# The second mixer of a two-block transformer kernel, rewritten: stick heads first, dilated scores in three float32r passes

## The chip, the cores and the metric

The kernel runs on one core of one Trainium2 chip. The metric is the device time of one execution in microseconds; the kernel before took 3473.2 us (median of three runs, 3472.29 to 3477.33). TensorE (PE) multiplies matrices, with its weight loads shown apart (PEld); VectorE (DVE), ScalarE (ACT) and GpSimd (POOL) do elementwise work; SyncE (SP) issues the weight transfers.

## The reference, cut to what matters

A sequence of 512 tokens of width 1024 passes two blocks of two layers. The change touches the mixer of the second block, `hybrid_mixer`, once in each of two layers:

```python
proj = h @ w_in                                 # 1024 -> 5120
# dilated: 12 heads of 64, four in each of three groups (window, dilation); q, k roped
for g, (window, dilation) in enumerate(((128, 1), (512, 4), (2048, 16))):
    o[g], lse[g] = dilated_window_attention(q_d[g], k_d[g], v_d[g], window, dilation)
o_dil = sum(softmax(lse, axis=0) * o)           # over the groups: 4 heads of 64
# stick breaking, 4 heads of 64:
z = q_s @ k_s.T / 8
after = reverse_cumsum(log_sigmoid(-z)) - log_sigmoid(-z)   # over earlier keys
o_sb = (exp(log_sigmoid(z) + after) where key < query) @ v_s
y = sigmoid(gate_dil) * (o_dil @ w_proj_dil) + sigmoid(gate_sb) * (o_sb @ w_proj_sb)
return y @ w_out
```

Everything is float32. A float32r product runs in one pass but keeps fewer bits, so the dense products are made of three: each operand is split into a high and a low part, and hi·hi, hi·lo and lo·hi are summed.

## The kernel before

Weights come as chunks of 128 x 1024. SP loads each into `wraw`, ACT copies it to `whi` (L63) and DVE subtracts to `wlo` (L64). One feature tile (128 features x 512 tokens) is `fm_block`: 8 k-tiles of three matmuls (`mm3a`, L177 to L179), summed in a PSUM bank `pa`. Token tiles (`tm`, `mm3b`, L183 to L185) fill four banks `pb` at once. PSUM has eight banks in two tags of four; dense work holds one tag, background work the other.

`mix2` walks its projections: the dilated q and k (names q0 to q5, k0 to k5; each `evac` runs `rope`: a DVE shuffle and a DVE multiplication that read the bank `pa`, then two POOL instructions), the values (`tm`), the stick q and k (sq, sk), and 16 gate tiles g0 to g15. `dilated(half)` and `stick` are generators in a background list: after every k-tile of dense work `tick` adds 640 ns of credit, and the generator runs on while it has credit, each `yield` naming its cost. So the order of every engine's queue is fixed when the program is built. `drain` runs what is left of the list at a stretch, before the last four gate tiles.

`dilated(half)` holds two heads, one on partitions 0 to 63 and one on 64 to 127, and works on them one after the other (s = 0, 1): scores (`far` twice, `near` twice) as float32 matmuls, which PE runs as two instructions each; transposes `pm` for the maxima, `pmt` to spread them, Exp on ACT, and `pod` with the values. `stick` takes four heads one after the other: scores `pz`, then per key block Abs, Exp and Ln on ACT and one DVE instruction (L1103 to L1106), sums with a triangular matrix into `pz` again, Exp, and `pos`. At the end, for each of eight tiles n, two products `pp` are multiplied by the gates g(n) and g(8+n) on DVE (L952), added on POOL (L954) and split into y's two parts, the input of `w_out`.

Of the kernel before, what the change touches and what calls it, by code (L numbers as in the profile page):

```python
# [11 lines left out]
F32 = mybir.dt.float32  # L12
# [8 lines left out]
T = 512  # L21
# [70 lines left out]
class Block:  # L92
# [769 lines left out]
    def mix2(self, l, next_gain, final):  # L862
        nc, a, ph = self.nc, self.a, self.phase
        self.n_scr = 8
# [46 lines left out]
        def to_v0_vsb(t, ps):  # L911
            nc.scalar.activation(v[:, t, 0:2, 0::2], heads(ps[:, :256]), AF.Copy)
            nc.scalar.activation(v_sb[:, t], ps[:, 256:], AF.Copy)

        def to_v12(t, ps):
            nc.scalar.activation(v[:, t, 2:6, 0::2], heads(ps), AF.Copy)

        o_dil = (ph.tile([128, 2, T], F32R, name="od_hi"), ph.tile([128, 2, T], F32R, name="od_lo"))
        o_sb = (ph.tile([128, 2, T], F32R, name="os_hi"), ph.tile([128, 2, T], F32R, name="os_lo"))
# [17 lines left out]
        def split_sum():  # L937
            y.append(self.fm_parts("fm", 17))
            self.split_to(*y[-1], sums.pop(0))

        for c in range(4):
            i, w = self.st.take()
            for j in range(2):
                n = 2 * c + j
                acc = []
                for s, src in enumerate((o_dil, o_sb)):
                    ps = self.bank(tag, "pp")
                    for k in range(2):
                        q = ((j * 2 + s) * 2 + k) * 128
                        self.mm3a(ps, [x[:, q:q + 128] for x in w], [x[:, k] for x in src], k == 0, k == 1)  # L950
# [19 lines left out]
    def dilated(self, half, fm, v, o_dil):  # L970
        nc = self.nc
        den, num = self.spare("den"), self.spare("num")
        mm = lambda out, lhsT, rhs: nc.tensor.matmul(out, lhsT, rhs, start=True, stop=True, skip_group_check=True)  # L973
        pair = self.window_kq[:, None, :].to_broadcast([128, 2, 256])
        for s in range(2):
            p = slice(64 * s, 64 * s + 64)
            q = [fm[f"q{2 * g + half}"][p] for g in range(3)]
            k = [fm[f"k{2 * g + half}"][p] for g in range(3)]
            mx = self.small.tile([128, 3, 4], F32, name="mx", bufs=2)
            lo, hi = slice(0, 64), slice(64, 128)  # L980

            def near(i):

                ps = self.bank(self.bg_tag, "pst")
                for b in (2 * i, 2 * i + 1):
                    n = min(256, T - b * 128)
                    mm(ps[:, (b % 2) * 256:(b % 2) * 256 + n], k[0][:, b * 128:(b + 1) * 128], q[0][:, b * 128:b * 128 + n])
                x = self.scratch("es")
                if i == 0:
                    f = lambda a: a.rearrange("p (a b) -> p a b", a=2)  # L990
                    nc.vector.tensor_add(f(x), f(ps), pair)
                else:
                    nc.vector.tensor_add(x[:, :384], ps[:, :384], self.window_kq3)
                return x

            def far(g, mask):
                ps = self.psum.tile([128, 4, 128], F32, name="pst", tag=self.bg_tag)
                for t in range(NT):
                    mm(ps[:, t], self.tokens(k[g], g, t), self.tokens(q[g], g, t))
                x = self.scratch("es").rearrange("p (t i) -> p t i", t=4)  # L1000
                nc.vector.tensor_add(x, ps, mask[:, None, :].to_broadcast([128, 4, 128]))
                return x

            def turned(blocks):
                ps = self.bank(self.bg_tag, "pm")
                for i, x in enumerate(blocks):
                    nc.tensor.transpose(ps[:, i * 128:(i + 1) * 128], x, self.ident)
                return ps

            def far_max(g, x):  # L1010
                ps = turned([x[:, t] for t in range(NT)])
                nc.vector.reduce_max(mx[:, g], ps.rearrange("p (t i) -> p t i", t=4), axis=AX)

            x1 = far(1, self.causal_kq)
            yield 900
            x2 = far(2, self.resid_kq)
            yield 900
            far_max(1, x1)
            yield 900
            x0 = near(0)  # L1020
            yield 900
            far_max(2, x2)
            nc.vector.tensor_max(mx[:, 1], mx[:, 1], mx[:, 2])
            yield 900
            x3 = near(1)
            yield 900
            of = lambda b, i: (x0 if b < 2 else x3)[:, (b % 2) * 256 + i * 128:(b % 2) * 256 + (i + 1) * 128]
            m = self.spare("m")
            ps = self.bank(self.bg_tag, "pmt")
            for t in range(NT):  # L1030
                nc.tensor.transpose(self.tokens(ps, 1, t), mx[:, 1, t:t + 1].to_broadcast([128, 128]), self.ident)
            nc.scalar.activation(m, ps, AF.Copy)
            yield 900
            ps = turned([of(0, 1), of(1, 0), of(1, 1), of(2, 0)])
            nc.vector.reduce_max(mx[:, 0, 1:3], ps.rearrange("p (t i) -> p t i", t=2), axis=AX)
            ps = turned([of(2, 1), of(3, 0), of(0, 0)])
            nc.vector.reduce_max(mx[:, 0, 3:4], ps[:, :256], axis=AX)
            nc.vector.reduce_max(mx[:, 0, 0:1], ps[:, 256:384], axis=AX)
            yield 1800
            ps = self.bank(self.bg_tag, "pmt")  # L1040
            for t in range(NT):
                nc.tensor.transpose(self.tokens(ps, 0, t), mx[:, 0, t:t + 1].to_broadcast([128, 128]), self.ident)
            nc.vector.tensor_max(m, m, ps)
            yield 900

            mt = m.rearrange("p (i t) -> p t i", t=4)
            tiles = []
            for g, x in ((1, x1), (2, x2)):
                nc.vector.tensor_sub(x, x, mt)
                nc.scalar.activation(x, x, AF.Exp, scale=0.125)  # L1050
                tiles.append([(x[:, t], t, g, None) for t in range(NT)])
            for x, bs in ((x0, (0, 1)), (x3, (2, 3))):
                n = 0
                tiles.append([])
                for b in bs:
                    w = min(256, T - b * 128)
                    nc.vector.tensor_sub(x[:, n:n + w], x[:, n:n + w], m[:, b * 128:b * 128 + w])
                    tiles[-1].append((x[:, n:n + w], b, 0, slice(b * 128, b * 128 + w)))
                    n += w
                nc.scalar.activation(x[:, :n], x[:, :n], AF.Exp, scale=0.125)  # L1060
            yield 2500
            po = self.bank(self.bg_tag, "pod")
            for i, tile_ in enumerate(tiles):
                for j, (x, t, g, cols) in enumerate(tile_):
                    lhsT = v[:, t, 2 * g + half, s:s + 2].rearrange("p a d -> p (a d)")
# [217 lines left out]
```

## Time and profile before

| | |
|---|---|
| median of the runs | 3473.2 us |
| profiled execution: its own time / its span | 3472.38 / 3470.6 us |
| PE busy | 98% of the span |
| chain that ended last | 90% PE, 4% DVE, 2% ACT |
| mean granted TensorE clock | 0.988 of full speed |
| background work of `mix2`, first dilated score to the end of the last stick head | 1665.72 to 1886.49 us and 2788.82 to 3009.48 us |

The profile is of one execution. A matmul's end is modelled, so two matmuls that follow each other overlap in it; what a group of them costs is read from its first start to the first start behind it.

### The profile page before, as it was taken

The page shows a single profiled execution, that of the slowest core. Times are in us where ns is not written, and L with a number is a line of the kernel's source. Part 1 is how long each engine was busy: PE and PEld are TensorE (multiplying, and loading weights), DVE is VectorE, ACT ScalarE, POOL GpSimd, SP SyncE. Part 2 cuts the span into 40 slices and gives each one's busy share as a digit, 9 for nine tenths or more (in the row PEclk, how much of TensorE's full clock was granted, in tenths as well). Part 3 has the DMA queues.
Part 4 walks back from the last instruction along what each step waited for, and adds up shares of the span by engine and source line. Part 5 has one row for each costly group of instructions (what it writes and reads, how often), then busy time and mean ns, then how long its engine had stood idle before and what let it go on. Part 6 is the DMA issues. An engine that isn't in the chain of part 4 may idle for free.

```text
span 3470.6 us, 39287 instructions
## 1 busy us (share of the span) xinstructions
PE 3389.0 (98%) x15984; PEld 2798.7 (81%) x15984; DVE 1512.5 (44%) x1989; ACT 1172.4 (34%) x1862; POOL 355.8 (10%) x412
## 2 busy tenths in 40 slices
PE   8899999989999999999999999999999999999999
PEld 6678888767888888888876888888888887688887
DVE  4655542565554343324543533333332454353332
ACT  4344432334443332222235332223222223533221
POOL 2421100242110000003200100000000320010000
PEclk9999999999999999999999999999999999999999
DMA  4122332312333233333111233323332311123332
GB/s 161 44 74 92 99 114 85 113 49 68 98 103 111 81 99 97 103 97 102 61 55 56 91 103 97 103 86 103 97 103 97 102 55 61 55 92 102 97 103 79
DMA packets 87188, 311.97 MB, mean 90 GB/s; under 512 B 10368, under 2 KB 11072, under 8 KB 87008
## 3 DMA queue, kind: packets, MB, share of 16 engines
q1 hardware_dynamic: 85536, 305.17, 27.1%
q0 software_dynamic: 1472, 4.30, 0.4%
q8 instruction: 126, 2.06, 0.2%
q14 instruction: 54, 0.44, 0.0%
HBM read 307.32 MB, written 2.10 MB: 89 GB/s over the span
## 4 chain that ended last, share of the span: by engine, by line
PE 90%; DVE 4%; ACT 2%; POOL 1%; issue 1%; DMA 1%; DVEq 0%; POOLq 0%; ACTq 0%; SPq 0%
PE pa L177 18%; PE pa L178 18%; PE pa L179 18%; PE pb L183 10%; PE pb L184 10%; PE pb L185 10%; PE pst L973 1%; PE pz L1079 1%; DVE wlo L64 1%; PE ph L220 1%; PE pod L1067 1%; ACT whi L63 1%; PE pos L1079 1%; DVE xn L210 1%; PE psc L662 0%
## 5 line engine op out<-in xcount | busy, mean ns | idle before, releaser
L64 DVE TENSOR_TENSOR wlo<-wraw,whi 128x1024 fp32r<-128x1024 f32 x556 | 706.9, 1273 | 1139.5 <-ACT whi L63 1138.1
L177 PE MATMUL pa<-h_hi,whi 128*128 128x512 f32 (+1 forms) x3072 | 1172.4, 382 | 2.0 <-ACT h_hi L162 2.0
L178 PE MATMUL pa<-h_lo,whi 128*128 128x512 f32 (+1 forms) x3072 | 1148.2, 374 | 2.7 <-DVE h_lo L163 2.7
L179 PE MATMUL pa<-h_hi,wlo 128*128 128x512 f32 (+1 forms) x3072 | 1147.3, 373 | 0.0
L63 ACT ACTIVATE whi<-wraw 128x1024 fp32r<-128x1024 f32 x556 | 585.2, 1053 | 723.1 <-PE pb L185 560.0
L177 PEld LDWEIGHTS pa<-h_hi,whi 128*128 128x128 f32 x3072 | 583.2, 190 | 112.4 <-issue 10.8
L179 PEld LDWEIGHTS pa<-h_hi,wlo 128*128 128x128 f32 x3072 | 582.5, 190 | 102.7
L178 PEld LDWEIGHTS pa<-h_lo,whi 128*128 128x128 f32 x3072 | 583.7, 190 | 97.2 <-DVE h_lo L163 4.3
L183 PE MATMUL pb<-whi,hid_hi 128*128 128x512 f32 x1056 | 411.8, 390 | 0.0
L184 PE MATMUL pb<-wlo,hid_hi 128*128 128x512 f32 x1056 | 410.9, 389 | 0.0
L185 PE MATMUL pb<-whi,hid_lo 128*128 128x512 f32 x1056 | 410.9, 389 | 0.0
L185 PEld LDWEIGHTS pb<-whi,hid_lo 128*128 128x128 f32 x1056 | 198.3, 188 | 41.3
L183 PEld LDWEIGHTS pb<-whi,hid_hi 128*128 128x128 f32 x1056 | 198.3, 188 | 40.9
L184 PEld LDWEIGHTS pb<-wlo,hid_hi 128*128 128x128 f32 x1056 | 198.3, 188 | 40.7
L438 ACT ACTIVATE hid_hi<-act 128x512 fp32r<-128x512 f32 x88 | 55.6, 632 | 383.9 <-DVE act L449 383.9
L201 POOL TENSOR_TENSOR rs<-ss 128x1 f32<-128x1 f32 x44 | 11.9, 271 | 1605.7 <-ACT sqs L191 1605.7
L449 DVE TENSOR_TENSOR act<-act,pa 128x512 f32<-128x512 f32 x88 | 60.4, 687 | 210.4 <-PE pa L179 210.4
L458 DVE SCALAR_TENSOR_TENSOR cv<-pa,cw,cv 128x511 f32<-128x511 f32 (+1 forms) x176 | 131.5, 747 | 16.0 <-ACT cv L456 12.9
L445 ACT ACTIVATE act<-pa 128x512 f32<-128x512 f32 x88 | 52.5, 597 | 246.6 <-PE pa L179 246.6
L183 PE MATMUL pb<-whi,h_hi 128*128 128x512 f32 x256 | 102.2, 399 | 5.4 <-ACT vg L618 3.1
L184 PE MATMUL pb<-wlo,h_hi 128*128 128x512 f32 x256 | 101.4, 396 | 1.2 <-DVE wlo L64 1.2
L185 PE MATMUL pb<-whi,h_lo 128*128 128x512 f32 x256 | 101.3, 396 | 0.0
(269 smaller groups left out, 2916.1 us busy)
## 6 DMA issues: line engine op xcount, KB each, us to landing
wraw<-w_ffn SPq DMA_DIRECT2D x264, 512.0 KB, 3.6
wraw<-w_mix SPq DMA_DIRECT2D x160, 512.0 KB, 3.6
wraw<-w_mlp SPq DMA_DIRECT2D x132, 512.0 KB, 3.6
X<-x SPq DMA_DIRECT2D x4, 512.0 KB, 7.7
gain<-norm_ffn SPq DMA_DIRECT2D x4, 512.0 KB, 4.5
out<-xn SPq DMA_DIRECT2D x8, 256.0 KB, 2.0
gain<-norm_mix_pre SPq DMA_DIRECT2D x2, 512.0 KB, 5.7
rope_da<-c_rope SPq DMA_DIRECT2D x2, 512.0 KB, 8.2
```

The source lines that it names most:

```text
L63: self.nc.scalar.activation(hi, t, AF.Copy)
L64: self.nc.vector.tensor_sub(lo, t, hi.bitcast(F32))
L177: mm(ps, w[0], h[0], start=first, stop=False)
L178: mm(ps, w[0], h[1], start=False, stop=False)
L179: mm(ps, w[1], h[0], start=False, stop=last)
L183: mm(ps, h[0], w[0], start=first, stop=False)
L184: mm(ps, h[0], w[1], start=False, stop=False)
L185: mm(ps, h[1], w[0], start=False, stop=last)
L438: nc.scalar.activation(hid[0][:, f], h, AF.Copy)
L449: nc.vector.tensor_mul(g, g, ps)
L458: nc.vector.scalar_tensor_tensor(c[:, s:], ps[:, :T - s], cw[:, j, i:i + 1], c[:, s:], op0=OP.mult, op1=OP.add)
L1079: mm = lambda out, lhsT, rhs, first: nc.tensor.matmul(out, lhsT, rhs, start=first, stop=True, skip_group_check=True)
```

## The change

The order of the projections (and of the weight chunks in `arrange`) is turned: stick q and k first, in the halves form, with `stick` queued at once; then the first values, six dilated tiles, `dilated(0)`, the other values, six dilated tiles, `dilated(1)`, gates. A dilated tile is roped into a `raw` tile and, at least 4500 ns of credit later, split into two float32r parts, for groups 1 and 2 with the tokens regrouped by residue, so that the scores read columns that lie side by side. Scores are three float32r passes, alternating between the two heads on partitions 0 to 63 and 64 to 127; every step of `dilated` serves both heads. All these tiles, the outputs and y share one tag of 24 buffers (before: 17, and the outputs apart). Stick's and dilated's last steps wait in the list until the values are there.

```diff
@@ mix2
-        self.n_scr = 8
+        self.n_scr = 9
-        new_fm = lambda name: ph.tile([128, T], F32, name="fm" + name, tag="fm", bufs=17)
+        new_fm = lambda name, dt=F32: ph.tile([128, T], dt, name="fm" + name, tag="fm", bufs=24)
+        self.two = lambda name: (new_fm(name + "h", F32R), new_fm(name + "l", F32R))
         def dil(name):
+            g = int(name[1]) // 2
+            turned = lambda x: x.rearrange("p (i r) -> p i r", r=4) if g else x
+            grouped = lambda x: x.rearrange("p (r i) -> p i r", r=4) if g else x
             def evac(ps):
-                fm[name] = new_fm(name)
-                self.rope(fm[name], ps, self.ROPE16, rope[:, 0], rope[:, 1])
+                raw = new_fm("raw")
+                self.rope(raw, ps, self.ROPE16, rope[:, 0], rope[:, 1])
+                def split():
+                    parts = self.two(name)
+                    self.split_to(*[grouped(x) for x in parts], turned(raw))
+                    fm[name] = parts
+                    fm["at"] = self.clock
+                self.after(4500, split)
...
-        self.fm([dil("q0"), dil("q2"), dil("q4"), dil("k0")], halves=True)
-        self.fm([dil("k2"), dil("k4")])
+        self.fm([plain("sq0", 0.125), plain("sk0", 1.0), plain("sq1", 0.125), plain("sk1", 1.0)], halves=True)
+        self.bg.work.append(self.stick(fm, v_sb, o_sb))
         self.tm(KD, 512, v_rows(0), to_v0_vsb, tag, tail=1)
+        self.fm([dil(n) for n in ("q0", "q2", "q4", "k0", "k2", "k4")])
+        self.bg.work.append(self.dilated(0, fm, v, o_dil))
         self.tm(KD, 512, v_rows(1), to_v12, tag, tail=1)
-        self.bg.work.append(self.dilated(0, fm, v, o_dil))
         self.fm([dil(n) for n in ("q1", "q3", "q5", "k1", "k3", "k5")])
         self.bg.work.append(self.dilated(1, fm, v, o_dil))
-        self.fm([plain("sq0", 0.125), plain("sq1", 0.125), plain("sk0", 1.0), plain("sk1", 1.0)])
-        self.bg.work.append(self.stick(fm, v_sb, o_sb))
         self.fm([plain(f"g{j}", 1.0) for j in range(12)])
         self.drain()
...
-            y.append(self.fm_parts("fm", 17))
+            y.append(self.two("y"))
@@ dilated
+        def scored(ps, g, key, query):
+            q, k = fm[f"q{2 * g + half}"], fm[f"k{2 * g + half}"]
+            for j, (a, b) in enumerate(((0, 0), (0, 1), (1, 0))):
+                for s, p in enumerate(rows):
+                    mm(ps[s], k[a][p, key], q[b][p, query], j == 0, j == 2)
...
-                    mm(ps[:, t], self.tokens(k[g], g, t), self.tokens(q[g], g, t))
+                scored([x[:, t] for x in ps], g, c, c)
```

The first place is PE's queue in layer 1, where the first dilated scores begin (`pst`; a row before is four float32 matmuls, `fmq`/`fmk` the q and k tiles, h and l their parts). Before:

```order
L179 MATMUL pa<-h_hi,wlo 128x512
L973 MATMUL pst<-fmq_11707,fmk_11810 128x128 x4
L177 MATMUL pa<-h_hi,whi 128x512
L178 MATMUL pa<-h_lo,whi 128x512
L179 MATMUL pa<-h_hi,wlo 128x512
L973 MATMUL pst<-fmq_11743,fmk_11847 128x128 x4
L177 MATMUL pa<-h_hi,whi 128x512
```

After:

```order
L185 MATMUL pb<-whi,h_lo 128x512
L986 MATMUL pst<-fmq2h,fmk2h 128x128 x2
L986 MATMUL pst<-fmq2l,fmk2h 128x128 x2
L986 MATMUL pst<-fmq2h,fmk2l 128x128 x2
L986 MATMUL pst<-fmq2h,fmk2h 128x128 x2
L986 MATMUL pst<-fmq2l,fmk2h 128x128 x2
L986 MATMUL pst<-fmq2h,fmk2l 128x128 x2
```

A far group is now twelve such rows, a pair of heads in each. Before, a layer has four series of 13 background groups of `dilated` in PE's queue, after two series of 18.

The second place is PE's queue in layer 2 where the list is drained, from the last scores of the fourth stick head to the first gate tile behind. Before:

```order
L1079 MATMUL pz<-fmsq_20074,fmsk_20191 128x128
L1079 MATMUL pz<-ab,tri 128x512 x2
L1079 MATMUL pz<-ab,tri 128x384 x2
L1079 MATMUL pz<-ab,tri 128x256 x2
L1079 MATMUL pz<-sp_20917,tri 128x128 x2
L1079 MATMUL pz<-ab,tri 128x384 x2
L1079 MATMUL pz<-ab,tri 128x256 x2
L1079 MATMUL pos<-sw,v_sb 64x512
L1079 MATMUL pos<-sw,v_sb 64x384
L1079 MATMUL pos<-sw,v_sb 64x256
L1079 MATMUL pos<-sw,v_sb 64x128
L177 MATMUL pa<-h_hi,whi 128x512
```

After, at the last background matmuls of the layer:

```order
L986 MATMUL pod<-es,v 128x256 x2
L177 MATMUL pa<-h_hi,whi 128x512
L178 MATMUL pa<-h_lo,whi 128x512
L179 MATMUL pa<-h_hi,wlo 128x512
L986 MATMUL pod<-es,v 128x256
L986 MATMUL pod<-es,v 128x128
L177 MATMUL pa<-h_hi,whi 128x512
```

Behind these stand 213 dense matmuls of gate tiles: nothing is left to drain. Before, the whole fourth head stood with no dense matmul between its steps.

The third place is DVE's queue in layer 2 at the last dilated tile before a `tm` (k4 in both). Brackets name the engines whose semaphores a row waits for. Before:

```order
L499 STREAM_SHUFFLE sh<-pa 128x512 [waits PE_49]
L500 TENSOR_TENSOR fmk_19256<-pa,rope 128x512
L64 TENSOR_TENSOR wlo<-wraw,whi 128x1024 [waits DMAHW2_49,Activation_49]
L499 STREAM_SHUFFLE sh<-pa 128x512 [waits PE_49]
L500 TENSOR_TENSOR fmk_19293<-pa,rope 128x512
```

After:

```order
L1148 SCALAR_TENSOR_TENSOR sp_19950<-pz,sp_19950 128x512 [waits PE_49,Activation_49]
L1148 SCALAR_TENSOR_TENSOR sp_19951<-pz,sp_19951 128x384 [waits PE_49,Activation_49]
L1148 SCALAR_TENSOR_TENSOR sp_19952<-pz,sp_19952 128x256 [waits DVE_49,PE_49,Activation_49]
L1148 SCALAR_TENSOR_TENSOR sp_19951<-pz,sp_19951 128x128 [waits Activation_49]
L163 TENSOR_TENSOR fmk2l<-fmraw,fmk2h 128x128x4 [waits Activation_49]
L499 STREAM_SHUFFLE sh<-pa 128x512 [waits PE_49]
L500 TENSOR_TENSOR fmraw<-pa,rope 128x512
```

The rope of k4 now stands behind the fourth stick head's four DVE steps and the split of k2. On PE, six dense matmuls follow that head's scores, then the `tm`, three matmuls for each of its four banks; the fourth of them takes k4's bank. The next place is DVE's queue at the gated sums of layer 2. Before:

```order
L952 TENSOR_TENSOR fmg2_20374<-fmg2_20374,pp_21169 128x512 [waits PE_49]
L952 TENSOR_TENSOR fmg10_20847<-fmg10_20847,pp_21177 128x512 [waits PE_49]
L163 TENSOR_TENSOR fm_lo_21187<-fmg1_20322,fm_hi_21186 128x512 [waits DVE_49,Activation_49]
L952 TENSOR_TENSOR fmg3_20437<-fmg3_20437,pp_21190 128x512 [waits PE_49]
L952 TENSOR_TENSOR fmg11_20897<-fmg11_20897,pp_21198 128x512 [waits PE_49]
```

After:

```order
L966 TENSOR_TENSOR fmg2_20850<-fmg2_20850,pp_21465 128x512 [waits PE_49]
L966 TENSOR_TENSOR fmg10_21236<-fmg10_21236,pp_21473 128x512 [waits PE_49]
L163 TENSOR_TENSOR fmyl_21483<-fmg1_20769,fmyh_21482 128x512 [waits Activation_49,Pool_49]
L966 TENSOR_TENSOR fmg3_20923<-fmg3_20923,pp_21486 128x512 [waits PE_49]
L966 TENSOR_TENSOR fmg11_21269<-fmg11_21269,pp_21494 128x512 [waits PE_49]
```

The low part of y(n) now waits for POOL: its buffer, by the program's addresses, is that of g(9+n), which POOL's addition of sum n+1 reads last. This holds for n = 0 to 3.

## Rows read from the trace of the kernel before

**Rows 1.** The page: busy time by engine; the group of the weight splits.

```profile
PE 3389.0 (98%) x15984; PEld 2798.7 (81%) x15984; DVE 1512.5 (44%) x1989; ACT 1172.4 (34%) x1862; POOL 355.8 (10%) x412
...
L64 DVE TENSOR_TENSOR wlo<-wraw,whi 128x1024 fp32r<-128x1024 f32 x556 | 706.9, 1273 | 1139.5 <-ACT whi L63 1138.1
```

**Rows 2.** Timeline of PE, mix2 of layer 2: start, length (us), instructions.

```profile
2788.82 2.24 PE L973 MATMUL pst<-fmq,fmk 64*128 64x128 f32 x8
2790.98 0.50 PE L177 MATMUL pa<-h_hi,whi 128*128 128x512 f32 x1
...
2798.37 1.13 PE L973 MATMUL pst<-fmq,fmk 64*128 64x256 f32 x4
2799.43 0.49 PE L177 MATMUL pa<-h_hi,whi 128*128 128x512 f32 x1
...
2802.15 0.92 PE L973 MATMUL pst<-fmq,fmk 64*128 64x256 f32 x4
2803.00 0.50 PE L177 MATMUL pa<-h_hi,whi 128*128 128x512 f32 x1
2803.34 0.40 PE L178 MATMUL pa<-h_lo,whi 128*128 128x512 f32 x1
2803.57 0.39 PE L179 MATMUL pa<-h_hi,wlo 128*128 128x512 f32 x1
```

**Rows 3.** Timeline of PE, scores of the first block's mixer.

```profile
83.31 0.33 PE L662 MATMUL psc<-fmk0h,fmq0h 64*128 64x128 f32 x2
83.48 0.28 PE L662 MATMUL psc<-fmk0l,fmq0h 64*128 64x128 f32 x2
83.59 0.27 PE L662 MATMUL psc<-fmk0h,fmq0l 64*128 64x128 f32 x2
83.80 0.29 PE L657 MATMUL psc<-masks 128*128 128x128 bf16 x2
84.01 0.39 PE L662 MATMUL psc<-fmk0h,fmq0h 64*128 64x256 f32 x2
84.24 0.29 PE L662 MATMUL psc<-fmk0l,fmq0h 64*128 64x256 f32 x2
84.36 0.28 PE L662 MATMUL psc<-fmk0h,fmq0l 64*128 64x256 f32 x2
84.57 0.50 PE L177 MATMUL pa<-h_hi,whi 128*128 128x512 f32 x1
```

**Rows 4.** Stretches of layer 2: busy by engine, granted clock, DMA share, GB/s.

```profile
2794.00:2798.00 4.00, 4.00 (x13) 3.22 (x13) 1.38 (x2) 0.00 (x0) 0.00 (x0) 0.57 0.00 0
2859.00:2866.00 7.00, 7.00 (x22) 5.25 (x22) 3.77 (x5) 1.84 (x3) 0.00 (x0) 0.51 0.24 75
2999.00:3006.00 7.00, 3.47 (x11) 2.83 (x12) 4.11 (x10) 4.41 (x12) 0.00 (x0) 0.51 0.00 1
```

**Rows 5.** Timeline, the drained stick head of layer 2; brackets: idle before, releaser.

```profile
2994.62 0.23 PE L1079 MATMUL pz<-masks 128*128 128x128 bf16 x1
2997.78 0.48 PE L1079 MATMUL pz<-fmsq,fmsk 64*128 64x128 f32 x2
...
3001.65 0.31 ACT L1105 ACTIVATE sp<-sp 128x128 f32<-128x128 f32 x1
...
3002.53 2.59 PE L1079 MATMUL pz<-ab,tri 128*128 128x512 f32 x6 [4.27 <-ACT ab L162]
3007.18 2.37 PE L1079 MATMUL pos<-sw,v_sb 128*64 128x512 f32 x8 [0.47 <-ACT sw L1126]
```

**Rows 6.** Groups by line, whole span: count, busy us, mean ns, idle before.

```profile
L163 DVE TENSOR_TENSOR fmk2l<-raw,fmk2h 128x512 fp32r<-128x512 f32 x2 | 1.4, 692 | 3.2 <-ACT fmk2h L162 3.2
L1049 DVE TENSOR_TENSOR es<-es,m 128x512 f32<-128x512 f32 x16 | 16.6, 1076 | 0.3
L954 POOL TENSOR_TENSOR fmg<-fmg,fmg 128x512 f32<-128x512 f32 x16 | 23.0, 1440 | 383.2 <-DVE fmg L952 382.5
L1042 PE MATMUL pmt<-ident,mx 128*128 128x128 f32 x32 | 4.9, 276 | 3.7 <-DVE mx L1038 3.7
```

More of the change, by code (lines that the diff above doesn't have):

```diff
@@ L971, in dilated, with near @@
         nc = self.nc
-        den, num = self.spare("den"), self.spare("num")
-        mm = lambda out, lhsT, rhs: nc.tensor.matmul(out, lhsT, rhs, start=True, stop=True, skip_group_check=True)
+        mm = lambda out, lhsT, rhs, start=True, stop=True: nc.tensor.matmul(out, lhsT, rhs, start=start, stop=stop,
+                                                                            skip_group_check=True)
+        names = [f"{a}{2 * g + half}" for a in "qk" for g in range(3)]
+        rows = [slice(64 * s, 64 * s + 64) for s in range(2)]
         pair = self.window_kq[:, None, :].to_broadcast([128, 2, 256])
[L975 to L987, printed above, removed]
+        while any(n not in fm for n in names):
+            yield 300
+        while self.clock < fm["at"] + 2500 and not self.forced:
+            yield 300
+        mx = [self.small.tile([128, 3, 4], F32, name="mx", bufs=2) for _ in range(2)]
+        def scored(ps, g, key, query):
[3 more added lines that the diff above has]
+                    mm(ps[s], k[a][p, key], q[b][p, query], j == 0, j == 2)
+        def near(i):
+            ps = [self.bank(self.bg_tag, "pst") for _ in rows]
+            for b in (2 * i, 2 * i + 1):
+                n = min(256, T - b * 128)
+                at = (b % 2) * 256
+                scored([x[:, at:at + n] for x in ps], 0, slice(b * 128, (b + 1) * 128), slice(b * 128, b * 128 + n))
+            xs = []
+            for s in range(2):
                 x = self.scratch("es")
@@ L990, in near @@
                     f = lambda a: a.rearrange("p (a b) -> p a b", a=2)
[L991 removed]
+                    nc.vector.tensor_add(f(x), f(ps[s]), pair)
                 else:
[L993 to L998, printed above, removed]
[L999 to L1002 removed]
@@ L1004, in turned @@
[L1004 to L1028, printed above, removed]
+                    nc.vector.tensor_add(x[:, :384], ps[s][:, :384], self.window_kq3)
@@ new lines, in near, with far @@
+                xs.append(x)
+            return xs
+        def far(g, mask):
+            ps = [self.psum.tile([128, 4, 128], F32, name="pst", tag=self.bg_tag) for _ in rows]
+            for t in range(NT):
+                c = slice(t * 128, (t + 1) * 128)
+                scored([x[:, t] for x in ps], g, c, c)
+            xs = []
+            for s in range(2):
+                x = self.scratch("es").rearrange("p (t i) -> p t i", t=4)
+                nc.vector.tensor_add(x, ps[s], mask[:, None, :].to_broadcast([128, 4, 128]))
+                xs.append(x)
+            return xs
@@ L1041, in dilated @@
[L1041 to L1048, printed above, removed]
+                nc.tensor.transpose(self.tokens(ps, g, t), mx[s][:, g, t:t + 1].to_broadcast([128, 128]), self.ident)
+            return ps
+        x1 = far(1, self.causal_kq)
@@ new lines, in dilated @@
+        yield 1800
+        x2 = far(2, self.resid_kq)
+        yield 1800
+        x0 = near(0)
+        yield 1800
+        x3 = near(1)
+        yield 1800
+        for s in range(2):
+            far_max(s, 1, x1[s])
+        yield 1800
+        for s in range(2):
+            far_max(s, 2, x2[s])
+            nc.vector.tensor_max(mx[s][:, 1], mx[s][:, 1], mx[s][:, 2])
+        yield 1800
+        m = [self.spare("m") for _ in range(2)]
+        of = lambda s, b, i: (x0 if b < 2 else x3)[s][:, (b % 2) * 256 + i * 128:(b % 2) * 256 + (i + 1) * 128]
@@ L1049, in dilated @@
+        yield 1800
+        for s in range(2):
+            nc.vector.tensor_max(m[s], m[s], maxima(s, 0))
+        yield 900
+        tiles = []
+        for s in range(2):
+            mt = m[s].rearrange("p (i t) -> p t i", t=4)
+            tiles.append([])
+            for g, x in ((1, x1[s]), (2, x2[s])):
                 nc.vector.tensor_sub(x, x, mt)
                 nc.scalar.activation(x, x, AF.Exp, scale=0.125)
-                tiles.append([(x[:, t], t, g, None) for t in range(NT)])
@@ L1073, in dilated @@
         nc.vector.tensor_mul(num, num, den)
[L1074 removed]
+        o_dil[half] = self.two("od")
+        self.split_to(*o_dil[half], num)
         yield 3500
@@ L1128, in stick @@
             yield 4000
+            while ("v", NT - 1) not in fm:
+                yield 300
             if s == 0:
```

66 lines of the change are left out of this document (41 added, 25 removed).

## The prediction

> **What bounds the kernel now.** I read the busy shares first, then the granted clock by stretch, then PE's timeline in `mix2`. PE is busy for 98% of the span and no other engine for half of it [rows 1]: the time is what PE's queue costs, and other engines count only where PE waits for them. Two neighbouring dense matmuls start 0.23 us apart [rows 2]; a dense k-tile of three is 0.69. The change leaves all dense matmuls as they are. So I look for what PE does in `mix2` beside them: the float32 scores [rows 2], stretches at half clock [rows 4], and the head that is drained with nothing beside it [rows 5]. All sums are per layer; there are two alike. They are made against the profiled execution's 3472.38 us, which is 0.8 under the median of the runs; the difference is left.
>
> **Scores.** Before, four dilated heads a layer (two halves, two heads) each pay two far groups of 2.16 us (2788.82 to the dense matmul at 2790.98) and near groups of 1.06 and 0.85 [rows 2]: 6.23 a head, 24.9 a layer. That is 0.27 us for each instruction of 128 columns. The three-pass form on two row groups stands already in the first block [rows 3]: a pair of matmuls, one for each head, starts 0.17 us before the next, then 0.11, and the last 0.21 before what follows; with 256 columns 0.23, 0.12 and 0.21. A far group is now twelve pairs: 0.17 + 10 x 0.11 + 0.21 = 1.48; the near groups are six pairs: 0.23 + 4 x 0.12 + 0.21 = 0.92, and about 0.90. So 4.78 for two heads, 9.6 a layer: **15.3 gained**. If each run of three pairs paid its own ends (0.49 and 0.56), it would be 4 x 0.49 for a far group, 6.1 for two heads and 12.7 gained; without ends at all 8.1 a layer and 16.8 gained. Since the pairs follow each other with nothing between, I take the middle one.
>
> **The drained head.** After, 213 dense matmuls stand behind the last background work (second piece of order rows), so the fourth stick head lies among dense work as the others do. Its own PE work stays; what goes is the wait of 4.27 and of 0.47 [rows 5], and the half clock that follows the first: from 3002.5 to 3006 PE works at 0.51 [rows 4], 3.5 x 0.49 = 1.7 lost. **6.4 gained**; 4.7 if that clock is lost elsewhere.
>
> **Small gains.** `pmt` waited 3.7 us in all for `mx` [rows 6], 1.85 a layer; it now stands two steps behind the maxima that it spreads, with a yield of 1800 between, so **1.85** goes (0 to 1.85). Each background group makes the dense matmul behind it 0.34 instead of 0.23 [rows 2]; 52 groups become 36: 16 x 0.11 = **1.8** (1 to 1.8).
>
> **The clock.** Each dilated head is followed by a stretch at half clock that begins some 5 us after its first far group: three heads as 2794 to 2798 (4 us at 0.57, 1.7 lost), one as 2859 to 2866 (7 at 0.51, 3.4 lost) [rows 4]: 8.6 a layer, at 1.2 instead of 2.4 GHz under dense matmuls. What stands ahead of every one is two far groups with one k-tile of dense work between them, in which PE starts a 128-column instruction only every 0.27 us. The new groups start one every 0.055 and have two or three k-tiles between them. The same form in the first block's mixer is not followed by it. I take **8.6** as gained; nothing would be gained if the fall has another cause (a rival below).
>
> **A new wait at k4.** The rope of k4 stands on DVE behind four steps of the fourth stick head (third piece of order rows), and these end with ScalarE's chain: first score at 2994.62, last Ln done at 3001.65 + 0.31, so 7.34 us after the first score [rows 5]. Then the split of k2: a ScalarE copy (0.7 as an estimate, a contiguous copy of this size being as long as the DVE step) and a DVE step that reads and writes with a stride. The row for a strided operand is 1.08, against 0.69 for a contiguous one [rows 6]; I take 1.08. Then shuffle and multiplication, 0.69 each by the same row. k4's bank is free at 7.34 + 0.7 + 1.08 + 1.38 = 10.5. PE is there earlier: 3.6 for the scores (2994.62 to 2997.78 + 0.48) and 15 dense matmuls at 0.23, 7.1. It waits 3.4, and 4.2 if both strided operands cost (1.46 on DVE, 1.1 on ScalarE): I take 3.8. A stall of 4.27 was followed by half clock, so 1.7 more: **5.5 lost** (2 to 8). Queued behind the waiting matmul is the whole `tm` and `dilated(0)`, all on PE. The dilated tiles beside heads 2 and 3 meet the same block of 7.3 us, but PE holds four banks and comes back to one after 16 us of dense work: these are hidden.
>
> **A new wait at the gated sums.** The low part of y(n) waits for POOL's addition of sum n+1 (last piece of order rows), so on DVE the steps no longer overlap POOL: two multiplications 1.38, POOL 1.44, y's low part 0.69, half a weight split 0.64 [rows 1, 6], about 0.1 for two handovers: 4.25 a sum, where PE needs 12 x 0.23 = 2.76. Four sums have such a buffer: 4 x 1.5 = 6.0 at most. PSUM lets PE run two sums ahead, which takes off some; before, DVE needed 2.7 of PE's 2.76, so there was little to take. **4.5 lost** (2 to 6).
>
> **The splits.** Twelve a layer, some 0.7 on ScalarE and 0.69 to 1.46 on DVE, beside 5.5 us of dense matmuls for each tile: hidden but for what the two waits already count. If DVE falls behind, `dilated(1)` waits for k5's parts: **0.5** (0 to 3). Queues of SP and POOL get the same instructions in another order; the weight chunks come in the new order of use, so no load is later.
>
> **Sum.** -15.3 - 6.4 - 1.85 - 1.8 - 8.6 + 5.5 + 4.5 + 0.5 = -23.45 a layer, -46.9 for two: 3472.4 - 46.9 = **3425 us**. With all terms at their good ends -32, 3408; with all at their bad ones but the clock's (12.7, 4.7, 0 and 1 gained, 8.6; 8, 6 and 3 lost) -10, 3452.
>
> **Rivals.**
> *The half clock stays.* For it: the fall comes also after waits of PE, as at 2999 [rows 4], and there will be new ones. Against it: all four stretches a layer follow far groups. It gives 3425 + 17 = 3442.
>
> *The loads bound the scores.* The pairs of 0.11 stand in runs of three whose first weights may lie ready; in a run of twelve each matmul may pay for its load. Between 0.055 [rows 3] and 0.27 [rows 2] the geometric mean is 0.12: 72 matmuls for two heads make 8.6, 17.3 a layer, 7.7 more than I took: 3425 + 15 = 3440. The Trainium skill, page "TensorE: Matmul & The Clock Gate", section "LDWEIGHTS (loading the stationary operand)", says that a load takes the time of its columns, P/1.2 ns, and that fewer rows make it no shorter; 107 ns for each of 72 would be an estimate of 7.7 for two heads and 3437 us. The trace speaks against loads one after the other: two matmuls with two loads start every 0.11 [rows 3].
>
> *The strided splits are slow.* For it: the one strided row has 0.38 on top of 0.69 [rows 6], with a single strided operand; the new DVE step has two. At 2.2 us on each engine k4's bank comes at 7.34 + 4.4 + 1.38 = 13.1, 2.3 later than taken, and DVE needs 2.2 + 1.38 + 1.27 = 4.85 of 5.5 us a tile, which leaves it 4 us for some 20 of `dilated(0)`: the parts of k5 come late and PE waits some 8 more. 3425 + 20 = 3445. The Trainium skill, page "SBUF — State Buffer", section "Door 1: The DMA port swizzle (why `[64,N]` ≈ `[32,N]`)", says that accesses which leave a 16-byte line each time pay a penalty. The row of 1.08 agrees: its operand steps by 16 bytes.
>
> *Slower than before.* One mechanism: DVE becomes the bound of the stretch of the ropes. Its work there is 12 tiles of 2.65 + s (s the split), three stick heads in which it is held for 7.3 and works 3.7, and about 20 for `dilated(0)`: 85 + 12 s. PE needs about 123 (12 x 5.5, 22 for the `tm`, some 35 of background). DVE passes PE at s = 3.2, and the gain is eaten from s = 5.1; at 5.5 the layer is 4.5 longer, 3481 us. Against it: that is five times the strided row.
>
> **How the numbers follow.** The forecast has 0.66, the clock 0.12, the loads 0.08, the slow splits 0.10, slower 0.03; 0.01 is for what I do not see. 3408 to 3447 holds the forecast's good end, the three middle rivals and most of the forecast's bad end. A measurement of this kernel tells about 0.2%, 7 us. Faster by more: 0.96; the same 0.01; slower 0.03.
>
> **What would show it.** Right: far groups of some 1.5 us; no stretch at half clock behind them; no stretch in `mix2` where stick matmuls stand without dense ones; one wait of PE of 3 to 5 us for a rope on DVE, at the first `pb` matmuls after k4; waits of about 1 us at `pp` for L966. Wrong: far groups over 2 us (loads), clock stretches in the same places, splits over 1.5 us with waits of `pst` for them, or a wait of PE that I did not name.

## The result, and the profile after

The changed kernel takes 3435.6 us (median of 4 runs, 3434.5 to 3436.8) against 3475.2 for the kernel before on the same chip: ratio 0.9889, interval [0.9877, 0.9901]. The profiled execution has a span of 3434.9 us against 3470.6. The forecast was 3425 in a range of 3408 to 3447: the side was right, but the time is 11 us above the forecast. By the two profiled spans 35.7 us are gained of the 46.9 that were forecast.

The page, busy time by engine [rows 1]: PE is still the bound, and it is PE's busy time that fell.

```profile
PE 3352.0 (98%) x16080; PEld 2770.5 (81%) x16080; DVE 1542.0 (45%) x2013; ACT 1192.8 (35%) x1886; POOL 356.3 (10%) x412
```

PE's timeline at the first far group of layer 2 (start, length, instructions) [rows 2]: for two heads (partitions 0 to 63 and 64 to 127, PE's two row groups here) it lasts 1.48 us, 2824.67 to 2826.15, as forecast; before it was 2.16 for one.

```profile
2824.67 0.33 PE L986 MATMUL pst<-fmq2h,fmk2h 64*128 64x128 f32 x2
2824.83 0.28 PE L986 MATMUL pst<-fmq2l,fmk2h 64*128 64x128 f32 x2
...
2825.95 0.27 PE L986 MATMUL pst<-fmq2h,fmk2l 64*128 64x128 f32 x2
2826.15 0.62 PE L183 MATMUL pb<-whi,h_hi 128*128 128x512 f32 x1
2826.61 0.40 PE L184 MATMUL pb<-wlo,h_hi 128*128 128x512 f32 x1
```

PE's waits, 2700 to 3080 us (sum, times, longest). The waits for `ab` at the drained head and for `mx` [rows 5, 6] are gone. The one of `pb` for L500 is new and was forecast, at its place and near its size; that at `pp` has grown from 0.4, less than forecast; those of `pst` for the parts of k3 and k5, 3.05 in all, were priced at 0.5; the small one at `pz` was not foreseen.

```profile
PE pb L183 <- DVE fmraw L500: 3.3, 1, 3.3
PE pp L177 <- DVE fmg L966: 2.1, 3, 1.5
PE pst L986 <- ACT fmk5h L162: 1.8, 1, 1.8
...
PE pst L986 <- DVE fmk5l L163: 0.7, 1, 0.7
PE pz L1121 <- DVE ab L163: 0.6, 2, 0.5
PE pst L986 <- DVE fmk3l L163: 0.6, 1, 0.6
```

Stretches of layer 2 (length; busy PE, PEld, DVE, ACT, POOL; granted clock). The half clock [rows 4] is gone behind all far groups but the one that waits. It now stands behind the two long waits, at k4 and at k5.

```profile
2806.00:2808.00 2.00, 2.00 (x5) 1.65 (x6) 2.00 (x2) 0.00 (x0) 1.92 (x2) 0.52 0.00 0
...
2902.00:2904.00 2.00, 2.00 (x13) 1.35 (x11) 2.00 (x4) 1.36 (x2) 0.00 (x0) 0.50 0.78 266
```

Timeline of DVE before the wait at k4: the last step of stick head 4, the split of k2, and the rope that frees the bank.

```profile
2802.63 0.29 DVE L1148 SCALAR_TENSOR_TENSOR sp<-pz,sp 128x128 f32<-128x128 f32 x1 [1.03 <-ACT sp L1147]
2803.60 1.06 DVE L163 TENSOR_TENSOR fmk2l<-fmraw,fmk2h 128x512 fp32r<-128x512 f32 x1 [0.68 <-ACT fmk2h L162]
...
2804.58 0.72 DVE L499 STREAM_SHUFFLE sh<-pa 128x512 f32<-128x512 f32 x1
2805.20 0.68 DVE L500 TENSOR_TENSOR fmraw<-pa,rope 128x512 f32<-128x512 f32 x1
```

The last matmul of k3's bank and that of k5's on PE (each tile is 24 matmuls, counted from the first tile of the mixer):

```profile
2878.11 0.39 PE L179 MATMUL pa<-h_hi,wlo 128*128 128x512 f32 x1
...
2883.55 0.39 PE L179 MATMUL pa<-h_hi,wlo 128*128 128x512 f32 x1
```

Timeline of DVE before the wait at k5. PE's far groups start at 2892.03 and need k3's and k5's parts.

```profile
2880.28 3.35 DVE L1113 RECIPROCAL den<-den 128x512 f32<-128x512 f32 x1
...
2885.13 0.69 DVE L163 TENSOR_TENSOR fmodl<-num,fmodh 128x512 fp32r<-128x512 f32 x1 [0.70 <-ACT fmodh L162]
...
2886.35 0.73 DVE L499 STREAM_SHUFFLE sh<-pa 128x512 f32<-128x512 f32 x1
...
2891.94 1.07 DVE L163 TENSOR_TENSOR fmk3l<-fmraw,fmk3h 128x512 fp32r<-128x512 f32 x1 [2.34 <-ACT fmk3h L162]
...
2892.93 0.73 DVE L499 STREAM_SHUFFLE sh<-pa 128x512 f32<-128x512 f32 x1
...
2898.43 1.06 DVE L163 TENSOR_TENSOR fmk5l<-fmraw,fmk5h 128x512 fp32r<-128x512 f32 x1 [2.27 <-ACT fmk5h L162]
```

To be read from it: k3's bank is full at 2878.5 and k5's at 2883.9, but their ropes start on DVE 8 and 9 us later. The tail of `dilated(0)` holds DVE until 2885.8, and k1's split follows; from 2876 to 2889.5 DVE is busy for 12.6 of 13.5 us. The rope of k3 starts at 2886.35, and k3's parts are ready only at 2893.0, since POOL's two instructions and ScalarE's copy lie between. The rope of k5 stands behind that split in DVE's queue, and its parts come at 2899.5. Ahead of each split DVE is idle for 2.3 us. So a queue that is late meets a long chain; DVE's mean load (39.9 of the 52 us from 2840 to 2892) shows neither.

### The profile page after: what moved, and what is told of

Its sections match the earlier page's. It is cut to its first block, busy times and chain, and to the rows that moved or that the text cites. A ratio compares the mean times of both kernels' runs of the same rounds, so it can differ in the third digit from the quotient of the medians.

```text
span 3434.9 us, 39516 instructions
## 1 busy us (share of the span) xinstructions
PE 3352.0 (98%) x16080; PEld 2770.5 (81%) x16080; DVE 1542.0 (45%) x2013; ACT 1192.8 (35%) x1886; POOL 356.3 (10%) x412
## 4 chain that ended last, share of the span: by engine, by line
PE 87%; DVE 6%; ACT 3%; POOL 2%; issue 2%; DMA 1%; DVEq 0%; POOLq 0%; ACTq 0%; SPq 0%
PE pa L177 17%; PE pa L178 17%; PE pa L179 17%; PE pb L183 10%; PE pb L184 10%; PE pb L185 10%; DVE wlo L64 1%; PE pz L1121 1%; PE ph L220 1%; PE pos L1121 1%; DVE xn L210 1%; PE pst L986 1%; DVE sh L499 1%; ACT whi L63 0%; PE psc L662 0%
```

## The experiments

Each ratio is to runs of the kernel before on the same chip, with its interval. Not all runs stand on one chip, so a small difference between two of them is read from the ratios. Eleven kernels ran.

### The waits

**Scores later** (changed kernel):

```diff
-        while self.clock < fm["at"] + 2500 and not self.forced:
+        while self.clock < fm["at"] + 7000 and not self.forced:
```

> The changed kernel with one number: the scores of a half wait until 7000 of credit after the last split instead of 2500, so PE comes to dilated(1) some 4.5 us of dense work later. Theory (the scores are early): in the changed kernel PE waits 0.59 + 1.80 + 0.66 = 3.05 us a layer for the parts of k3 and k5, and some 1.5 of half clock follow; both go, 9 us for two layers, 3435.6 - 9 = 3426.5, no L986 wait left and no stretch at half clock near the second half's scores. Rival (VectorE is behind in this stretch and PE would wait for it anywhere): the waits come back as waits for mx, es or a rope, and the time stays at 3434 to 3437.

Measured 3425.6, 0.9867 [0.9853, 0.9882]. No wait of `pst` is left, nor the half clock behind it, and no wait came in its place. DVE has not caught up: k3's bank is full at 2872.2 in this trace, and its rope starts at 2880.01, again 8 us later. The scores stood too early for that, and PE has other work to do first.

**Fourth stick head later** (changed kernel):

```diff
-            yield 1000
+            yield 3500 if h == 2 else 1000
```

> The changed kernel with one number: 3500 of credit instead of 1000 behind the third stick head, so that the rope of k4 stands on VectorE ahead of the fourth head's four steps. Theory (the wait of 3.34 us at the fourth pb bank is these steps, and the half clock behind it the wait's): 3.3 + 1.7 a layer go, 10 for two, 3435.6 - 10 = 3425.5; if the split of k2 still holds the rope, some 0.6 of the wait stays. Rival (the split of k2 with its stride, ScalarE copy and VectorE step together 2.1 us, is what holds the rope): at least 2 of the 3.3 us stay and the half clock with them, 3433.

Measured 3425.3, 0.9863 [0.9847, 0.9880]. The wait at `pb` is gone altogether, so the split of k2 alone does not hold PE, and its half clock went with it.

**Other buffers for y** (changed kernel):

```diff
-            y.append(self.two("y"))
+            part = lambda x: ph.tile([128, T], F32R, name=x, tag="scr", bufs=self.n_scr)
+            y.append((part("yh"), part("yl")) if len(y) < 4 else self.two("y"))
```

> The changed kernel with y's parts of the first four gated sums in buffers of the scratch tag, which nothing reads any more, instead of the buffers that the gates leave. Theory (y's low part waits for POOL's addition through its buffer): the waits at pp fall from 2.15 us a layer to 0.4 or less and the first matmul of a sum starts 0.1 earlier: 2.6 a layer, 5.2 for two, 3430.4. Rival (VectorE's own work a sum, two multiplications, a split and half a weight split, is what PE waits for): the waits stay over 1.5 a layer and the time is 3434 to 3436.

Measured 3433.2, 0.9886 [0.9872, 0.9901]: by the time alone not told from the changed kernel. The waits at `pp` fall from 2.1 to 0.5 a layer, and in layer 1 the whole layer becomes 2.6 shorter, as expected. In layer 2 of the profiled execution half clock took it back: a stretch behind a stick head's scores, where PE waited for nothing, is new, and the one behind the waits for k3 and k5 lasts longer than in the changed kernel (there the slice from 2900 to 2904 is at 0.71):

```profile
2716.00:2720.00 4.00, 4.00 (x13) 2.97 (x12) 1.68 (x3) 3.35 (x9) 0.00 (x0) 0.63 0.32 124
...
2900.00:2904.00 4.00, 4.00 (x18) 2.84 (x18) 2.48 (x6) 1.54 (x2) 0.00 (x0) 0.50 0.39 133
```

So the cause is shown by the trace, and the size by one layer.

**All three.**

> The three edits together (scores of a half later, fourth stick head later, y in scratch buffers). Theory (three separate waits of PE, each with its own cause): the gains add, 9 + 10 + 5.2 = 24, 3411. Rival (one shared cause, VectorE behind in the whole mixer): together they bring no more than the best of them, 3425.

Measured 3410.0, 0.9821 [0.9807, 0.9836]. PE's waits in layer 2, all that is left:

```profile
PE pa L178 <- DVE h_lo L163: 0.7, 2, 0.3
PE pa L177 <- ACT h_hi L162: 0.5, 2, 0.2
PE pp L177 <- DVE fmg L967: 0.4, 1, 0.4
PE pz L1122 <- DVE ab L163: 0.4, 1, 0.4
```

Over both mixers no slice of 4 us is below full clock any more. In layer 1 of the profiled executions the three edits alone take away 5.9, 5.8 and 2.6 us, and together 14.2: there the gains add, so these are three separate waits. By the ratios of the whole the three gains add up to some 18 us, and together it is 24, which intervals of some 5 us each don't tell apart. Half clock went with the first two; behind the waits at `pp` there was none.

### The scores

The next four change one thing in the kernel with all three edits (3410.0).

**Float32 scores on the regrouped columns** (the low parts are left out of the scores):

```diff
-            for j, (a, b) in enumerate(((0, 0), (0, 1), (1, 0))):
-                for s, p in enumerate(rows):
-                    mm(ps[s], k[a][p, key], q[b][p, query], j == 0, j == 2)
+            for s, p in enumerate(rows):
+                mm(ps[s], k[0].bitcast(F32)[p, key], q[0].bitcast(F32)[p, query])
```

> On top of the three edits together (3410): the scores as one float32 matmul per block and head instead of three float32r passes, on the same regrouped columns; the low parts are left out of the scores. It asks what made the far groups of before slow, 0.27 us an instruction of 128 columns, and the clock fall behind them. Theory L (the weight loads with a stride: 328 ns each in before, 186 here): without the stride an instruction of 128 columns starts every 0.11, a far group of two heads is 16 x 0.11 + 0.1 = 1.9, the near groups are 1.1 (the row groups overlap) to 2.1, no half clock follows: 3412 to 3423. Theory P (float32 itself has the pace of 0.27): 4.3 a far group, half clock behind it, 25 a layer: 3460.

Measured 3412.8, 0.9835 [0.9819, 0.9850]. PE's timeline at the first far group:

```profile
2809.88 1.16 PE L987 MATMUL pst<-fmq2h,fmk2h 64*128 64x128 f32 x16
2810.97 0.63 PE L183 MATMUL pb<-whi,h_hi 128*128 128x512 f32 x1
```

1.09 us for two heads: float32 is not slow here, it is faster than the three passes (1.48). The theory had 1.9, without the two row groups side by side. No half clock follows. Theory L.

**No regrouping:**

```diff
-            turned = lambda x: x.rearrange("p (i r) -> p i r", r=4) if g else x
-            grouped = lambda x: x.rearrange("p (r i) -> p i r", r=4) if g else x
+            turned = grouped = lambda x: x
...
-                c = slice(t * 128, (t + 1) * 128)
+                c = slice(t, None, 4)
```

> On top of the three edits together (3410): the split writes the tokens in their own order, and the scores of groups 1 and 2 read every fourth column, for the weights too. Theory L (a weight load with the stride bounds a far group): far groups grow from 1.5 to between 3.9 (0.16 a matmul, if the loads of the two row groups overlap) and 6.5 (0.27), 10 to 20 a layer, and half clock comes back behind them: 3430 to 3480, although the splits fall from 1.07 to 0.69. Rival (the passes set the pace, and the strided splits cost as much as they save): 3407 to 3412.

Measured 3430.8, 0.9881 [0.9866, 0.9896]: 21 us lost. The first far group of layer 2, now 2.98 us:

```profile
2820.28 0.49 PE L986 MATMUL pst<-fmq2h,fmk2h 64*128 64x128 f32 x2
2820.58 0.42 PE L986 MATMUL pst<-fmq2l,fmk2h 64*128 64x128 f32 x2
...
2822.91 0.41 PE L986 MATMUL pst<-fmq2h,fmk2l 64*128 64x128 f32 x2
2823.26 0.63 PE L183 MATMUL pb<-whi,h_hi 128*128 128x512 f32 x1
```

A pair starts every 0.233 instead of 0.11. Its weight loads (least, median, longest ns):

```profile
L986 PEld LDWEIGHTS pst<-fmq2h,fmk2h x8: 304/326/326, 2820.3 to 2822.4; 64*128 64x128 f32 x8
```

The same tile with all three edits:

```profile
L987 PEld LDWEIGHTS pst<-fmq2h,fmk2h x8: 182/188/188, 2809.3 to 2810.3; 64*128 64x128 f32 x8
```

And in the run without regrouping the half clock is back behind the far groups (stretch, busy times, granted clock):

```profile
2828.00:2832.00 4.00, 4.00 (x13) 2.86 (x11) 1.29 (x2) 0.60 (x1) 0.00 (x0) 0.57 0.15 58
```

Every fourth float32 column as weights takes 326 ns to load where columns side by side take 188. That stride stood in the kernel before, and its loads show it:

```profile
L973 PEld LDWEIGHTS pst<-fmq,fmk x192: 182/328/330, 1665.7 to 2902.3; 64*128 64x128 f32 x192
```

The Trainium skill, page "SBUF — State Buffer", section "Door 1: The DMA port swizzle (why `[64,N]` ≈ `[32,N]`)", says that accesses which go to another 16-byte line each time pay a penalty; these loads agree, with 326 for 188. The prediction weighed that rule for the splits alone.

In these runs q, the moving operand, has or lacks the stride together with the weights. The two `tm` of the changed kernel part the two: the second reads every fourth token as weights, under a moving operand that lies side by side. First `tm`, then second, in layer 2:

```profile
L183 PEld LDWEIGHTS pb<-whi,h_hi x32: 186/188/192, 2715.2 to 2742.1; 128*128 128x128 f32 x32
...
L183 PEld LDWEIGHTS pb<-whi,h_hi x32: 308/310/333, 2800.1 to 2839.1; 128*128 128x128 f32 x32
```

A dense matmul starts every 0.227 us in the first and every 0.237 in the second, where a pair takes 0.233 here. So the stride of the weights alone lengthens the load, and it is enough for about this pace; what a strided moving operand costs by itself, no run shows.

**Three matmuls of one head, then three of the other:**

```diff
-            for j, (a, b) in enumerate(((0, 0), (0, 1), (1, 0))):
-                for s, p in enumerate(rows):
+            for s, p in enumerate(rows):
+                for j, (a, b) in enumerate(((0, 0), (0, 1), (1, 0))):
```

> On top of the three edits together (3410): the same three passes, but first all of one head, then all of the other, so that neighbouring matmuls use the same row group. Theory (the two row groups work side by side, a pair in 0.11): one after the other each matmul of 128 columns starts 0.11 behind the one before it, a far group is 24 x 0.11 + 0.1 = 2.7 instead of 1.5, the near groups 1.7 instead of 0.9: 8 a layer, 3426, and if this pace is slow enough for the clock to fall some 3 to 8 a layer more. Rival (the pace of 0.055 a matmul is that of 128 columns at full clock, with or without the alternation): 3409 to 3412.

Measured 3411.1, 0.9825 [0.9810, 0.9839]: no loss, against my theory. The rows tell why:

```profile
2811.04 0.33 PE L987 MATMUL pst<-fmq2h,fmk2h 64*128 64x128 f32 x2
2811.21 0.28 PE L987 MATMUL pst<-fmq2l,fmk2h 64*128 64x128 f32 x2
```

The same name twice in a row is the two heads, though in the program two other matmuls stand between them: they still ran side by side. So this run could not tell the two row groups from one, and the next was made.

**Head by head** (`scored` takes one head, and `far` and `near` loop over the heads outside the blocks):

```diff
-            for t in range(NT):
-                c = slice(t * 128, (t + 1) * 128)
-                scored([x[:, t] for x in ps], g, c, c)
+            for s in range(2):
+                for t in range(NT):
+                    c = slice(t * 128, (t + 1) * 128)
+                    scored(ps[s][:, t], g, c, c, s)
```

> On top of the three edits together (3410): all twelve matmuls of one head's score group, then all twelve of the other's. With three and three (the run before) the records of the two heads still start in pairs, 10 ns apart. Theory S (PE runs two row groups side by side when their matmuls stand near each other): far apart they run one after the other, each row group at 0.11 a matmul: 24 x 0.11 + 0.1 = 2.7 a far group, 1.4 to 1.7 a near one, 7 a layer, 3424. Rival (0.055 is the pace of any contiguous matmul of 128 columns, one row group or two): 1.5 as before, 3410.

Measured 3421.7, 0.9843 [0.9827, 0.9860]. The first far group, 2.43 us:

```profile
2813.37 0.33 PE L987 MATMUL pst<-fmq2h,fmk2h 64*128 64x128 f32 x1
2813.54 0.27 PE L987 MATMUL pst<-fmq2l,fmk2h 64*128 64x128 f32 x1
...
2814.32 0.38 PE L987 MATMUL pst<-fmq2h,fmk2h 64*128 64x128 f32 x2
2814.49 0.32 PE L987 MATMUL pst<-fmq2l,fmk2h 64*128 64x128 f32 x2
2814.60 0.32 PE L987 MATMUL pst<-fmq2h,fmk2l 64*128 64x128 f32 x2
2814.71 0.27 PE L987 MATMUL pst<-fmq2h,fmk2h 64*128 64x128 f32 x1
...
2815.80 0.73 PE L183 MATMUL pb<-whi,h_hi 128*128 128x512 f32 x1
```

One row group takes a matmul every 0.11; two run side by side at the seam, where the last three of one head meet the first three of the other. Theory S, with a saving of three matmuls that it did not foresee.

### One part alone

**Order only** (kernel before; the chunks in `arrange` and `stick`'s wait for the values go with it):

```diff
-        self.fm([dil("q0"), dil("q2"), dil("q4"), dil("k0")], halves=True)
-        self.fm([dil("k2"), dil("k4")])
+        self.fm([plain("sq0", 0.125), plain("sk0", 1.0), plain("sq1", 0.125), plain("sk1", 1.0)], halves=True)
+        self.bg.work.append(self.stick(fm, v_sb, o_sb))
         self.tm(KD, 512, v_rows(0), to_v0_vsb, tag, tail=1)
+        self.fm([dil(n) for n in ("q0", "q2", "q4", "k0", "k2", "k4")])
...
```

> The kernel before with the new order of the projections alone: stick heads first, float32 scores, one head at a time, no split. Theory (the terms are separate): the drained head goes, 6.2 a layer; the rope of k4 still stands behind the fourth stick head's four steps, but without the split of k2 (2.1), so PE waits some 1.2 and half a stretch of half clock follows, 2.5 a layer; the half clock behind the float32 far groups stays: -3.7 a layer, 3472 - 7 = 3465. Rival (the new wait eats the drained head's gain): 3470 to 3473, and the rewritten scores then carry the whole gain of the change.

Measured 3463.9, 0.9972 [0.9961, 0.9984]: 10 us gained, 7 expected (nine runs from 3459.3 to 3470.1; the profiled one is the longest). PE's waits in its layer 2: the drained head's are gone, `pmt` waits as before, and the wait at k4 is there, shorter without the split of k2 (3.3 in the changed kernel):

```profile
PE pmt L1042 <- DVE mx L1038: 1.9, 3, 1.1
PE pb L183 <- DVE fmk L500: 1.6, 1, 1.6
```

No half clock follows this wait of 1.6, in either layer.

**Regrouping only** (kernel before; `raw` of groups 1 and 2 in a scratch buffer, and each half waits for its copies):

```diff
...
+                def copy():
+                    fm[name] = raw
+                    if int(name[1]) > 1:
+                        fm[name] = new_fm(name)
+                        nc.scalar.activation(fm[name].rearrange("p (r i) -> p i r", r=4),
+                                             raw.rearrange("p (i r) -> p i r", r=4), AF.Copy)
+                    fm["at"] = self.clock
+                self.after(4500, copy)
...
-                    mm(ps[:, t], self.tokens(k[g], g, t), self.tokens(q[g], g, t))
+                    c = slice(t * 128, (t + 1) * 128)
+                    mm(ps[:, t], k[g][:, c], q[g][:, c])
```

> The kernel before with one edit: the q and k tiles of groups 1 and 2 are copied into groups of residues by ScalarE, so the float32 scores read columns that lie side by side; old order, one head at a time, drained stick head as before. Theory L (the weight load with the stride set the pace and the clock fell for that pace): an instruction of 128 columns starts every 0.11 to 0.13 instead of 0.27, a far group is 1.0 to 1.1 instead of 2.16 (8 a layer: 8.9), and the half clock behind them goes (8.6): 3472 - 35 = 3437. If the pace falls and the clock does not stay up: 3454. Rival (one head at a time in float32 keeps its 0.27): 3472.

Measured 3445.5, 0.9914 [0.9898, 0.9929]: 30 of the change's 39 us, with float32, the old order and one head at a time. The first far group of layer 2:

```profile
2778.86 1.15 PE L982 MATMUL pst<-fmq,fmk 64*128 64x128 f32 x8
2779.94 0.50 PE L177 MATMUL pa<-h_hi,whi 128*128 128x512 f32 x1
```

Its weight loads:

```profile
L982 PEld LDWEIGHTS pst<-fmq,fmk x192: 182/188/189, 1670.9 to 2879.8; 64*128 64x128 f32 x192
```

1.08 instead of 2.16 [rows 2], and no stretch at half clock is left behind a far group, only the one behind the drained head.

**No split at all** (three edits, float32 scores, and a ScalarE copy that regroups; nothing left out):

```diff
-                    parts = self.two(name)
-                    self.split_to(*[grouped(x) for x in parts], turned(raw))
-                    fm[name] = parts
+                    fm[name] = raw
+                    if g:
+                        fm[name] = new_fm(name)
+                        nc.scalar.activation(grouped(fm[name]), turned(raw), AF.Copy)
```

> On top of the three edits together (3410): float32 scores and no split at all; a ScalarE copy regroups the raw tiles of groups 1 and 2, group 0 is used as it is. Nothing is left out of the computation. Far groups 1.1 instead of 1.5, near ones some 0.1 longer, as in the float32 run: 0.65 a layer less on PE; 24 VectorE steps of 0.69 to 1.07 go, all of them hidden. Theory (only the regrouping is needed): 3408 to 3411, the same within what can be measured. Rival (the three passes are needed): over 3415.

Measured 3411.6, 0.9814 [0.9799, 0.9829]. This and the three edits alone (0.9821) are not told apart; both beat the changed kernel, whose interval ends at 0.9877, by some 25 us.

## Why the prediction was right, and where it was off

Layer 2, from the last `ph` transposes ahead of `mix2` to the first behind it, was 370.6 us and is 352.7; layer 1, 370.7 and 354.0. Each distance from one start to the next on PE, waits taken out and listed by themselves, gives for layer 2:

| term | forecast | measured | from |
|---|---|---|---|
| scores | -15.3 | -14.7 | `pst` 25.2 to 10.5, of which 0.65 is half clock |
| drained head | -6.4 | -5.9 | waits 4.27 and 0.47, `pz` -1.1 |
| `pmt` | -1.85 | -1.6 | wait 1.87 gone, its transposes +0.3 |
| groups and clock | -10.4 | -7.0 | `pa` -8.8, `pm` -0.85, `pb` +2.6 |
| k4 | +5.5 | +5.0 | wait 3.34; eight matmuls in 3.59 instead of 1.88 |
| gated sums | +4.5 | +2.6 | waits 2.13 less 0.37, first matmul of a sum +0.1 |
| splits late | +0.5 | +3.05 | three waits of `pst` for k3 and k5 |
| stick's parts | 0 | +0.6 | two waits of `pz` |
| sum | -23.45 | -17.9 | |

**The mis-sized terms.** "If DVE falls behind, `dilated(1)` waits for k5's parts: 0.5 (0 to 3)" was priced by DVE's load over the whole stretch. What counts is when a part is ready: DVE's queue comes to the ropes of k3 and k5 8 and 9 us after their banks are full, and then 6.6 us lie between the start of a rope on DVE and the end of its split (2892.93 to 2899.49), through POOL and ScalarE, with k5's rope behind k3's split. The 3.05 are followed by half clock, which the forecast gave to the wait at k4 and not to this one; in layer 2 it costs 1.5 in the rows of `pst` and `pa`, in layer 1 about 2.9. Moving the scores showed it: 9 us expected, 9 in the two layers of that trace (352.7 to 349.7, 354.0 to 348.1), though in layer 2 half clock at other places (0.74 from 2768 to 2772) ate part of it.

The 36 background groups for 52 were priced by their effect on feature tiles. Part of them now stands in the second `tm`, whose weights are every fourth token of h: there the dense matmul behind a group takes 0.44 to 0.46, as 2826.15 to 2826.61 above, and not 0.34. With all waits gone `pb` is still 2.2 a layer above the kernel before. This was argued from rows, not tested by a run.

The gated sums cost 2.6 and not 4.5; the place and the buffer were right, as the other buffers for y showed. The prediction had named PE's running ahead as what takes something off; how much that is, no run tested. The waits at `pz`, 0.6, it had not named. Its good ends add up to 31.5 a layer and not 32, so 3409 and not 3408.

**Right in size, wrong in cause.** The scores came out within 0.6 us, because the first block's rows [rows 3] were the right yardstick. But the prediction put the price on "the three-pass form on two row groups". The runs say otherwise: the stride was the price (regrouping alone 1.08 a far group for one head, all but the regrouping 2.98 for two), and by the loads of the second `tm` that of the weights; the two row groups help by about 1 us a far group (2.43 against 1.48), as long as the heads stand near each other; and the three passes give nothing (1.09 in float32). The rival that the loads bound the scores was thought of for the new kernel; it was the old one that they bound.

**The clock.** All four stretches a layer behind far groups went, as forecast, and regrouping alone takes them all away while the drained head keeps its own. In the runs with the stride they are there: 0.57 in the one without regrouping, and behind seven of the eight heads in the one of the order alone. With head by head one came back, 2816 to 2820 at 0.57, behind a far group of 2.43. What stays open: some executions have a stretch at half clock behind the scores of a stick head with no wait of PE, as 2708 to 2712 at 0.57 in the last kernel, and others of nearly the same order have none.

**Order and rivals.** The order alone is worth 10 us, the regrouping alone 30; that is 40 by adding two runs, and the change gives 39. So what two heads a step and the fewer groups may have brought was eaten by the new waits, as it seems; no run has these two alone. Some 24 us come back with the three edits. The strided splits took 1.05 to 1.12 on DVE (1.08 taken) and 1.06 to 1.14 on ScalarE (0.7 to 1.1 taken). They are hidden but in the chains ahead of the two waits: at k4 PE waits 3.3 with the split of k2 and 1.6 without it, in the run of the order alone. The rival with 2.2 was off. The slower one did not come near: over the stretch of the ropes DVE kept up, if up to 9 us late.

## What to carry to other kernels

Read the weight loads by themselves: where one takes 326 ns beside others of 188, look whether the stationary operand is read with a stride; here one copy into neighbouring columns paid for all its uses. Price a handover by the latency of its chain and by what stands in order ahead of it, not by how busy the engines are. Add what the clock takes: waits of 3.0 and 3.3 us a layer cost 1.5 to 2.9 more at half clock here, one of 1.6 none. When a rewrite changes layout, precision and order at once, run each alone before the next is built on it.

## What the runs showed of the hardware

- Two matmuls on different row groups ran side by side with two others between them in the program, and at a seam three deep. The Trainium skill, page "TensorE: Matmul & The Clock Gate", section "The mechanism", says that matmuls start in program order, without reordering; the rows of 2811.04 and 2814.32 speak against it, if names are put to records rightly.
- Weights read as every fourth float32 column took 304 to 336 ns to load, neighbouring ones 182 to 192, under a moving operand with the stride (326 in the run without regrouping) and under one without it (310 in the second `tm`).
- A float32 product of 128 columns with 64 rows, as two instructions, kept the pace of 0.11 us an instruction and row group, that of float32r.
